# One transposition and split of the keys per head pair, with copies on GpSimd's queue

## The chip, the cores and the metric

The kernel runs on one core of one Trainium2 chip. The metric is the device time of one execution in microseconds (us), stated as the median of several. One core has five engines that each work through their own instruction list in order: TensorE (PE in the rows; its weight loads are PEld), VectorE (DVE), ScalarE (ACT), GpSimd (POOL) and SyncE (SP), which issues most of the transfers. They meet only at semaphores.

## The reference, cut to what matters

Two layers of a trunk over 512 tokens (256 latent and 256 context) of width 1024. In each layer one input projection feeds three branches; two of them are attentions with heads of 64:

```python
z = u @ w_in                                   # columns: qa ka va | qb kb vb | pool | gates
ka = rms_norm(ka.reshape(B, N, NA_HEADS, HEAD_DIM), kn_a)      # 6 heads: 3 pairs
kb = rms_norm(kb.reshape(B, N, GQA_KV_HEADS, HEAD_DIM), kn_b)  # 2 key heads: 1 pair
# branch A: neighbourhood attention of the latent queries over all keys, with a bias
# branch B: grouped attention, three query heads to one key head, rotary on the latent tokens
s = q @ k.T ;  p = softmax(s) ;  y = p @ v
# branch C: pooled means of a 256-wide part of z over windows of 2, 4, 8, 16 tokens, times w_pool
m = ga * (ya @ w_br_a) + gb * (yb @ w_br_b) + gc * (yc @ w_br_c)
```

Then come an output projection and a SwiGLU feed-forward part. So a layer has four pairs of key heads (three of branch A, one of branch B), and the two layers have eight.

## The kernel before, in words

All large products are float32 made of two rounded parts: each operand is split into a high part (rounded by ScalarE) and a low part (the rest, by VectorE), and one product is three matmuls, high by high, low by high, high by low (L227 to L229 for the projections). Weights come by SyncE's transfers as `raw`; ScalarE writes `wh` (L133) and VectorE `wl` (L145). A list of jobs (ORDER) fixes the order of the projections; TensorE's matmuls for them are the main line of the program. Beside it run side generators, of which three are active at a time. After every group of matmuls one of them may take a step; `yield 3` means that it rests for three such ticks. A scheduler then fixes one list for each engine, and an instruction waits until what it needs is there.

The projection of a pair ends with `chunk_end` (L691): GpSimd turns sums of squares into `rs` (L696, L697, a power), and a side generator is added, `prep_na` (L725, branch A) or `prep_kb` (L780, branch B). `prep_na` multiplies keys by `rs` and writes them to `zkn` (L746). TensorE needs the turned keys of each head on both halves of the 128 partitions: a query head is laid out with its high part on one half and its low part on the other (`q_stacks`, L702), so that one matmul over 128 partitions against `ksh` (L876) and one against `ksl` (L877) give all the products. Before the change that layout is made by writing each head twice into `zkn` (two head copies beside each other, the `dup` loop), and by transposing once for each head: `k_stack` (L717) makes four transposes of 128x128 (L720) into one PSUM tile `kt`, then a split into `ksh` (ScalarE, L237) and `ksl` (VectorE, L242, or L239 where there is no scale). `prep_kb` does the same for the key pair of branch B, after norm, gain (L791) and rotation (L774, L777, L796).

GpSimd also does the pooled means (`pool_mix`: sums on L1040, scaling on L1064, subtraction on L1066, whose result ScalarE splits into `plh`, and TensorE multiplies by `wpoolh` into `pool`), rotates the queries of branch B (`prep_qb`: L774, L777, L820), and issues the bias loads `rpb` (L389). Its list, too, is worked off in order.

The attention itself (`attend_x` and `attend_ctx`, L858 and L918) has the score matmuls `s` on L876, L877 and, for the context queries of the first layer, on L926 and L927.

Of the kernel before, what the change touches and what calls it, by code (L numbers as in the profile page):

```python
# [8 lines left out]
F32 = mybir.dt.float32  # L9
F32R = mybir.dt.float32r  # L10
AF = mybir.ActivationFunctionType
ALU = mybir.AluOpType
AX = mybir.AxisListType

P = 128
# [3 lines left out]
TOK = 512  # L19
UNIT = 512  # L20
DEPTH = 2
HD = 64
# [9 lines left out]
ROW_N1, ROW_N2, ROW_PS, ROW_QA, ROW_KA = 48, 56, 64, 66, 67  # L32
# [142 lines left out]
class Trunk:  # L175
# [538 lines left out]
            res.append(t)  # L714
        return res

    def k_stack(self, srcs, scale):  # L717
        ps = self.u("kt")
        for i, s in enumerate(srcs):
            self.nc.tensor.transpose(ps[:, i * P : (i + 1) * P], s, self.ident)  # L720
        k = self.g2([P, TOK], "ks")
        self.split(k[0], k[1], ps, scale)
        return k

    def prep_na(self, l, p, st):  # L725
        nc = self.nc
        rpb = [self.load_bias(l, 2 * p + h) for h in range(2)]
        yield 4
        z, rs = st["z"], st["rs"]
        nq = 2 if l == DEPTH - 1 else 4  # L730
        zq = self.g([P, 4, P], name="zqn")
        zk = [self.g([P, 2, 2, 2, HD], name="zkn") for _ in range(2)]

        def zz(t, c):
            return z[t][:, :, c * P : (c + 1) * P].rearrange("p t (h d) -> p t h d", d=HD)

        def rr(t, c):
            return rs[:, 2 * t : 2 * t + 2, 2 * c : 2 * c + 2].unsqueeze(3).to_broadcast([P, 2, 2, HD])

        for t in range(2):  # L740
            if 2 * t < nq:
                o = zq[:, 2 * t : 2 * t + 2, :].rearrange("p t (h d) -> p t h d", d=HD)
                nc.vector.tensor_tensor(o, zz(t, 0), rr(t, 0), ALU.mult)
        for dup in range(2):
            for t in range(2):
                nc.vector.tensor_tensor(zk[t][:, :, :, dup, :], zz(t, 1), rr(t, 1), ALU.mult)  # L746
        yield 3
        cols = self.cols[l]
        q = self.q_stacks([zq[:, i, :] for i in range(nq)], cols[:, ROW_QA : ROW_QA + 1])
        yield  # L750
        ks = []
        for h in range(2):
            ks.append(
                self.k_stack(
                    [zk[t // 2][:, t % 2, h, :, :].rearrange("p a d -> p (a d)") for t in range(4)],
                    cols[:, ROW_KA : ROW_KA + 1],
                )
            )
            yield
        self.side.add(self.attend_x(l, ("a", p), q, ks, st["v"], rpb))  # L760
        if l < DEPTH - 1:
            self.side.add(self.attend_ctx(l, ("a", p), q, ks, st["v"]))
# [17 lines left out]
    def prep_kb(self, l, p, st):  # L780
        nc = self.nc
        yield 4
        z, rs = st["z"], st["rs"]
        z3 = z.rearrange("p t (h d) -> p (t h) d", d=HD)
        r3 = rs.rearrange("p t h -> p (t h)").unsqueeze(2).to_broadcast([P, 8, HD])
        nc.vector.tensor_tensor(z3, z3, r3, ALU.mult)
        zk = [self.g([P, 2, 2, 2, HD], name="zkn") for _ in range(2)]
        o = zk[1].rearrange("p t h a d -> p (t h) a d")
        x = z[:, 2:4, :].rearrange("p t (h d) -> p (t h) d", d=HD).unsqueeze(2).to_broadcast([P, 4, 2, HD])
        gk = self.gain[:, 1, :].unsqueeze(1).unsqueeze(1).to_broadcast([P, 4, 2, HD])  # L790
        nc.vector.tensor_tensor(o, x, gk, ALU.mult)  # L791
        for tt in range(2):
            t2 = self.rotate(nc.vector, z[:, tt, :], 2, 1, tt)
            x = z[:, tt, :].rearrange("p (h d) -> p h d", d=HD).unsqueeze(2).to_broadcast([P, 2, 2, HD])
            t2 = t2.rearrange("p (h d) -> p h d", d=HD).unsqueeze(2).to_broadcast([P, 2, 2, HD])
            nc.vector.tensor_tensor(zk[0][:, tt, :, :, :], x, t2, ALU.add)  # L796
        yield 3
        ks = []
        for h in range(2):
            ks.append(  # L800
                self.k_stack([zk[t // 2][:, t % 2, h, :, :].rearrange("p a d -> p (a d)") for t in range(4)], 1.0)
            )
            yield
        self.kb = (ks, st["v"])
        self.done.add(("kb", l))

# [715 lines left out]
```

## Time and profile before

| | |
|---|---|
| median of 3 runs | 1257.27 us (1256.89 to 1258.57) |
| profiled execution | 1254.5 us, its span 1252.7 us |
| mean granted TensorE clock in it | 0.983 of full speed |
| TensorE busy | 1205.3 us, 96% of the span |
| VectorE busy | 934.3 us, 75% |
| ScalarE busy | 656.0 us, 52% |
| GpSimd busy | 163.2 us, 13% |

Times in the rows are from the span's start, so 1.8 us of the profiled execution lie outside it. A row of the timeline gives the start, the length and, in brackets, how long the engine had stood idle and which instruction released it. An engine with a high busy share sets the time only where others wait for it, and an engine with a low share can still hold them up at single places.

### The profile page before, as it was taken

How to read it: one execution, taken by the hardware profiler on the slowest of the kernel's cores; microseconds unless marked ns; L12 is line 12 of the kernel's file. 1: busy time of each engine (PE TensorE's matmuls, PEld its weight loads, DVE VectorE, ACT ScalarE, POOL GpSimd, SP SyncE). 2: the span in 40 equal slices, each digit the busy share in tenths (PEclk: the TensorE clock that was granted, in tenths of full speed). 3: DMA queues.
4: the chain of work that ended last, by engine and by line, in shares of the span. 5: the costliest groups of instructions: out<-in, count | busy, mean ns of one | idle time of the engine just before them, and what ended most of it. 6: DMA issues, size and time to landing. Idle time of an engine off the chain costs nothing.

```text
span 1252.7 us, 20829 instructions
## 1 busy us (share of the span) xinstructions
PE 1205.3 (96%) x7307; PEld 1075.9 (86%) x7307; DVE 934.3 (75%) x1736; ACT 656.0 (52%) x1421; POOL 163.2 (13%) x215
## 2 busy tenths in 40 slices
PE   7999999999999889999999999989999999999998
PEld 2788889788887788888887888988999999999998
DVE  5867789999998987776677434778889778755563
ACT  4755588575333543332222333566878667654553
POOL 3253400101100110000000000275011101000000
PEclk9899999999999989999999999989999999999999
DMA  8732244343555444556666333233344565666663
GB/s 291 205 81 69 83 137 129 87 147 122 182 164 188 124 143 135 180 174 226 215 213 213 100 98 102 79 114 92 88 112 113 159 194 161 171 185 184 183 183 97
DMA packets 164612, 185.47 MB, mean 148 GB/s; under 512 B 12840, under 2 KB 148636, under 8 KB 164508
## 3 DMA queue, kind: packets, MB, share of 16 engines
q1 hardware_dynamic: 162700, 181.50, 47.2%
q0 software_dynamic: 1808, 2.66, 1.8%
q8 instruction: 57, 0.93, 0.3%
q14 instruction: 47, 0.39, 0.1%
HBM read 183.05 MB, written 1.05 MB: 147 GB/s over the span
## 4 chain that ended last, share of the span: by engine, by line
PE 73%; DVE 10%; DMA 6%; ACT 5%; issue 4%; POOL 2%; SPq 1%; DVEq 0%; ACTq 0%; POOLq 0%
PE acc L227 22%; PE acc L228 22%; PE acc L229 22%; DMA mraw<-in_w_mod_dram 3%; DVE wl L145 2%; PE y L853 2%; DMA whole<-in_w_mod_dram 2%; ACT wh L133 1%; DVE macc L491 1%; PE pt L899 1%; ACT p L842 1%; DVE xT L1146 1%; PE s L876 1%; PE s L877 1%; DMA raw<-in_w_ff_dram 1%
## 5 line engine op out<-in xcount | busy, mean ns | idle before, releaser
L133 ACT ACTIVATE wh<-raw 128x512 fp32r<-128x512 f32 (+2 forms) x512 | 306.7, 612 | 352.6 <-PE acc L228 251.5
L145 DVE TENSOR_TENSOR wl<-raw,wh 128x512 fp32r<-128x512 f32 (+2 forms) x512 | 343.0, 679 | 164.9 <-ACT wh L133 161.2
L227 PE MATMUL acc<-uh,wh 128*128 128x256 f32 (+1 forms) x1104 | 371.6, 338 | 7.8 <-DVE b L1259 3.6
L229 PE MATMUL acc<-uh,wl 128*128 128x256 f32 (+1 forms) x1104 | 369.7, 336 | 4.7 <-DVE wl L145 4.7
L228 PE MATMUL acc<-ul,wh 128*128 128x256 f32 (+1 forms) x1104 | 369.8, 336 | 1.8 <-DVE ul L591 1.8
L227 PEld LDWEIGHTS acc<-uh,wh 128*128 128x128 f32 x1104 | 211.7, 193 | 28.7 <-issue 3.8
L229 PEld LDWEIGHTS acc<-uh,wl 128*128 128x128 f32 x1104 | 212.4, 193 | 25.1 <-DVE wl L145 4.9
L228 PEld LDWEIGHTS acc<-ul,wh 128*128 128x128 f32 x1104 | 212.8, 193 | 21.3 <-DVE ul L591 2.0
L491 DVE SCALAR_TENSOR_TENSOR macc<-mraw,sf,macc 128x1024 f32<-128x1024 f32 x112 | 143.6, 1289 | 56.2 <-DMA mraw<-in_w_mod_dram 56.2
L227 PE MATMUL acc<-wh,uh 128*128 128x384 f32 (+1 forms) x304 | 100.5, 331 | 4.6 <-ACT uh L1323 4.4
L228 PE MATMUL acc<-wl,uh 128*128 128x384 f32 (+1 forms) x304 | 98.8, 325 | 4.2 <-DVE wl L145 4.2
L229 PE MATMUL acc<-wh,ul 128*128 128x384 f32 (+1 forms) x304 | 98.8, 325 | 0.0
L576 POOL TENSOR_TENSOR ut<-xT,rstd 128x256 f32<-128x256 f32 x30 | 25.0, 862 | 530.3 <-DVE rstd L556 411.9
L227 PE MATMUL acc<-hh,wh 128*128 128x512 f32 (+1 forms) x216 | 75.7, 351 | 0.0
L229 PE MATMUL acc<-hh,wl 128*128 128x512 f32 (+1 forms) x216 | 75.6, 350 | 0.0
L228 PE MATMUL acc<-hl,wh 128*128 128x512 f32 (+1 forms) x216 | 75.5, 350 | 0.0
L227 PEld LDWEIGHTS acc<-wh,uh 128*128 128x128 f32 x304 | 59.2, 195 | 6.1 <-ACT uh L1323 4.5
L228 PEld LDWEIGHTS acc<-wl,uh 128*128 128x128 f32 x304 | 59.4, 195 | 5.5 <-DVE wl L145 4.5
L229 PEld LDWEIGHTS acc<-wh,ul 128*128 128x128 f32 x304 | 59.2, 195 | 0.6 <-DVE ul L1325 0.6
L842 ACT ACTIVATE p<-s,m 128x512 f32<-128x512 f32 (+1 forms) x72 | 44.3, 619 | 13.9 <-DVE m L882 5.5
L227 PE MATMUL acc<-h,wh 128*128 128x256 f32 x176 | 50.3, 286 | 0.0
L228 PE MATMUL acc<-h,wh 128*128 128x256 f32 x176 | 49.8, 283 | 0.0
(279 smaller groups left out, 2180.5 us busy)
## 6 DMA issues: line engine op xcount, KB each, us to landing
raw<-in_w_ff_dram SPq DMA_DIRECT2D x264, 256.0 KB, 3.0
mraw<-in_w_mod_dram SPq DMA_DIRECT2D x80, 512.0 KB, 4.2
raw<-in_w_in_dram SPq DMA_DIRECT2D x112, 256.0 KB, 2.8
raw<-in_w_in_dram SPq DMA_DIRECT2D x144, 64.0 KB, 2.0
whole<-in_w_mod_dram SPq DMA_DIRECT2D x32, 256.0 KB, 5.3
raw<-in_w_out_dram SPq DMA_DIRECT2D x32, 256.0 KB, 3.0
raw<-in_w_in_dram SPq DMA_DIRECT2D x16, 192.0 KB, 2.7
raw<-in_w_br_c_dram SPq DMA_DIRECT2D x8, 256.0 KB, 3.0
```

What stands on the lines that cost most here:

```text
L133: self.nc.scalar.activation(hi[:, :n], self.raw[i][:, :n], AF.Copy)
L145: self.nc.vector.tensor_tensor(lo[:, :n], self.raw[i][:, :n], self.hi[i][:, :n].bitcast(F32), ALU.subtract)
L227: mm(out, st[0], mv[0], start=start, stop=False)
L228: mm(out, st[0], mv[1], start=False, stop=False)
L229: mm(out, st[1], mv[0], start=False, stop=stop)
L491: nc.vector.scalar_tensor_tensor(acc[v], w, c, acc[v], ALU.mult, ALU.add)
L576: eng.tensor_tensor(ts[i][:, 0, :], self.xT[:, kt, c], self.r0[:, c], ALU.mult)
L842: nc.scalar.activation(pt, ps, AF.Exp, scale=-1.0, bias=m, accum_out=s[:, 0:1])
L853: mm(o, st, t[:, kt % 2, :], start=kt == 0 and i == 0, stop=kt == n - 1 and i == 1)
L876: nc.tensor.matmul(ps, st, ks[h][0], start=True, stop=False)
L877: nc.tensor.matmul(ps, st, ks[h][1], start=False, stop=True)
L899: nc.tensor.transpose(ps[:, kt * P : (kt + 1) * P], pr[h, qt][:, kt * P : (kt + 1) * P], self.ident)
```

## The change

`k_stack`, called twice for a pair, becomes `k_stacks`, called once. The keys of the two heads stand side by side in `zkn` (in `prep_kb` in the norm's own tile `z`), each once; four transposes turn both heads at a time, so head 0 lands on partitions 0 to 63 and head 1 on 64 to 127; one split writes `kk`, high and low. After a rest of two ticks eight transfers on GpSimd's queue (L731 of the changed kernel) copy each head's 64x512 block, 128 KB, from `kk` to both halves of its own `ks` tiles: two heads, high and low, two halves. With eight pairs that is 64 transfers and 8.4 MB. Removed are 32 transposes, eight splits (ScalarE and VectorE one each), and half of the doubled writes to `zkn` on VectorE.

```diff
-    def k_stack(self, srcs, scale):
+    def k_stacks(self, srcs, scale):
         ps = self.u("kt")
         for i, s in enumerate(srcs):
             self.nc.tensor.transpose(ps[:, i * P : (i + 1) * P], s, self.ident)
-        k = self.g2([P, TOK], "ks")
-        self.split(k[0], k[1], ps, scale)
-        return k
+        both = self.g2([P, TOK], "kk")
+        self.split(both[0], both[1], ps, scale)
+        yield 2
+        res = []
+        for h in range(2):
+            k = self.g2([P, TOK], "ks")
+            for t, b in zip(k, both):
+                src = b[h * HD : (h + 1) * HD, :].bitcast(F32)
+                for half in range(2):
+                    self.nc.gpsimd.dma_start(out=t[half * HD : (half + 1) * HD, :].bitcast(F32), in_=src)
+            res.append(k)
+        yield
+        return res
...
-        zk = [self.g([P, 2, 2, 2, HD], name="zkn") for _ in range(2)]
+        zk = self.g([P, 4, P], name="zkn")
...
-        for dup in range(2):
-            for t in range(2):
-                nc.vector.tensor_tensor(zk[t][:, :, :, dup, :], zz(t, 1), rr(t, 1), ALU.mult)
+        for t in range(2):
+            o = zk[:, 2 * t : 2 * t + 2, :].rearrange("p t (h d) -> p t h d", d=HD)
+            nc.vector.tensor_tensor(o, zz(t, 1), rr(t, 1), ALU.mult)
...
-        ks = []
-        for h in range(2):
-            ks.append(self.k_stack(...))
-            yield
+        ks = yield from self.k_stacks([zk[:, t, :] for t in range(4)], cols[:, ROW_KA : ROW_KA + 1])
...
-            nc.vector.tensor_tensor(zk[0][:, tt, :, :, :], x, t2, ALU.add)
+            nc.vector.tensor_tensor(z[:, tt, :], z[:, tt, :], t2, ALU.add)
```

Where the copies come to stand in GpSimd's list matters. In the rows below, a name with a number is one buffer of a tile. In the first layer, after the power of the first `rs` of branch B (`rs` of 128x8), GpSimd goes on with the second half of the pooled means; before:

```order
L696 TENSOR_SCALAR rs_1089<-ss_886 128x8
L658 MEMSET ss_1289 128x24
L697 TENSOR_TENSOR rs_1089<-rs_1089,mhalf 128x8
L1040 TENSOR_TENSOR s_173_1150<-vp_874 128x271
L1040 TENSOR_TENSOR s_174_1151<-s_173_1150 128x268
```

The same place of GpSimd's list in the changed kernel (x2 is two instructions alike, one for each half of the partitions; L1034 is the old L1040):

```order
L696 TENSOR_SCALAR rs_1086<-ss_886 128x8
L658 MEMSET ss_1290 128x24
L697 TENSOR_TENSOR rs_1086<-rs_1086,mhalf 128x8
L731 DMA ksh_1110<-kkh_1083 64x512 x2
L731 DMA ksl_1111<-kkl_1084 64x512 x2
L731 DMA ksh_1116<-kkh_1083 64x512 x2
L731 DMA ksl_1117<-kkl_1084 64x512 x2
L1034 TENSOR_TENSOR s_173_1150<-vp_874 128x271
L1034 TENSOR_TENSOR s_174_1151<-s_173_1150 128x268
```

The eight copies of the first pair have come between the power and the second half of the pooled means.

TensorE's list at the product of that second half with `wpoolh`, before:

```order
L720 MATMUL kt_1232<-ident,zkn_1217 128x128
L720 MATMUL kt_1241<-ident,zkn_1217 128x128
L227 MATMUL pool_1250<-plh_1148,wpoolh_882 128x512
L227 MATMUL acc_1296<-wh_1179,uh_124 128x384
L228 MATMUL pool_1250<-pll_1149,wpoolh_882 128x512
L229 MATMUL pool_1250<-plh_1148,wpooll_883 128x512
```

And in the changed kernel:

```order
L721 MATMUL kt_1230<-ident,zk_888 128x128
L229 MATMUL acc_1296<-wh_1179,ul_125 128x384
L227 MATMUL pool_1258<-plh_1148,wpoolh_882 128x512
L721 MATMUL kt_1230<-ident,zk_888 128x128 x3
L228 MATMUL pool_1258<-pll_1149,wpoolh_882 128x512
L229 MATMUL pool_1258<-plh_1148,wpooll_883 128x512
```

The product stands where it stood: right after the first transposes of branch B's keys, and ahead of all that follows on TensorE.

In the second layer, at the first pair of branch A, GpSimd's list has the rotation of two query tiles and then waits for the next `ss`; before:

```order
L774 TENSOR_TENSOR rot_1120_8891<-zqn_1119_8889,rope_1050_8332 128x12x16 [waits DVE_49]
L774 TENSOR_TENSOR rot_1120_8891<-zqn_1119_8889,rope_1050_8332 128x12x16
L777 TENSOR_TENSOR zqn_1119_8889<-zqn_1119_8889,rope_1050_8332 128x384 [waits Pool_49]
L820 TENSOR_TENSOR zqn_1119_8889<-zqn_1119_8889,rot_1120_8891 128x384 [waits Pool_49]
L696 TENSOR_SCALAR rs_1151_9086<-ss_1105_8824 128x8 [waits DVE_49]
L697 TENSOR_TENSOR rs_1151_9086<-rs_1151_9086,mhalf_81 128x8 [waits Pool_49]
```

In the changed kernel (L777, L780 and L814 are the old L774, L777 and L820; what an instruction waits for stands in brackets, DMASW being an earlier transfer of this queue):

```order
L777 TENSOR_TENSOR rot_1119_8892<-zqn_1118_8890,rope_1049_8333 128x12x16
L780 TENSOR_TENSOR zqn_1118_8890<-zqn_1118_8890,rope_1049_8333 128x384 [waits Pool_49]
L814 TENSOR_TENSOR zqn_1118_8890<-zqn_1118_8890,rot_1119_8892 128x384 [waits Pool_49]
L731 DMA ksh_1128_8980<-kkh_1126_8964 64x512 [waits DMASW3_49,Activation_49]
L731 DMA ksh_1128_8980<-kkh_1126_8964 64x512 [waits DMASW4_49]
L731 DMA ksl_1129_8981<-kkl_1127_8965 64x512 [waits DMASW5_49,DVE_49]
L731 DMA ksl_1129_8981<-kkl_1127_8965 64x512 [waits DMASW6_49]
L731 DMA ksh_1130_8986<-kkh_1126_8964 64x512 [waits DMASW7_49]
```

The copies stand behind the last rotation. On TensorE the first score matmul of this pair had 24 projection matmuls between the first `kt` and itself before, and has 36 of them now.

## Rows read from the trace of the kernel before

**Rows 1.** The page: engine totals, and shares of the chain that ended last

```profile
PE 1205.3 (96%) x7307; PEld 1075.9 (86%) x7307; DVE 934.3 (75%) x1736; ACT 656.0 (52%) x1421; POOL 163.2 (13%) x215
...
PE 73%; DVE 10%; DMA 6%; ACT 5%; issue 4%; POOL 2%; SPq 1%; DVEq 0%; ACTq 0%; POOLq 0%
```

**Rows 2.** Groups by form (busy us, mean ns, idle before) of what the change thins

```profile
L720 PE MATMUL kt<-ident,zkn 128*128 128x128 f32 x64 | 10.5, 281 | 2.5 <-DVE zkn L746 2.0 <-DVE zkn L796 0.5
L746 DVE TENSOR_TENSOR zkn<-z,rs 128x256 f32<-128x256 f32 x24 | 12.9, 592 | 0.0
L242 DVE SCALAR_TENSOR_TENSOR ksl<-kt,cols,ksh 128x512 fp32r<-128x512 f32 x12 | 8.9, 748 | 0.9 <-ACT ksh L237 0.6
```

**Rows 3.** Issues on GpSimd by line: ns min/median/max; the last row is landing

```profile
L376 POOL DMA_DIRECT2D wpool<-in_w_pool_dram x8: 518/529/560, 42.4 to 818.1; - x8
DMA to landing us min/median/max: 2.2/2.4/3.6
L389 POOL DMA_DIRECT2D rpb<-in_rpb_a_dram x24: 592/606/683, 44.6 to 951.6; - x24
DMA to landing us min/median/max: 3.2/4.2/6.4
```

**Rows 4.** TensorE's timeline behind the first pair's second four transposes, first layer

```profile
89.35 0.50 PE L227 MATMUL acc<-uh,wh 128*128 128x512 f32 x1 [0.63 <-DVE v L239]
```

**Rows 5.** GpSimd's timeline there, and ScalarE's split of the pooled means

```profile
89.97 0.20 POOL L696 TENSOR_SCALAR rs<-ss 128x8 f32<-128x8 f32 x1 [6.09 <-DVE ss L687]
...
91.95 0.63 POOL L1040 TENSOR_TENSOR s<-vp 128x271 f32<-128x271 f32 x1
...
103.11 1.07 POOL L1066 TENSOR_TENSOR r<-r,vp 128x256 f32<-128x256 f32 x1
104.22 0.42 ACT L237 ACTIVATE plh<-r 128x256 fp32r<-128x256 f32 x1 [3.02 <-POOL r L1066]
```

**Rows 6.** TensorE's timeline at the pooled product

```profile
105.33 0.41 PE L720 MATMUL kt<-ident,zkn 128*128 128x128 f32 x2 [0.46 <-DVE zkn L796]
105.50 0.47 PE L227 MATMUL pool<-plh,wpoolh 128*128 128x512 f32 x1
```

**Rows 7.** TensorE after an idle stretch; window: length, busy (count), clock, transfers' share, GB/s

```profile
830.09 0.69 PE L228 MATMUL acc<-wl,uh 128*128 128x384 f32 x1 [4.21 <-DVE wl L145]
830.00:835.00 5.00, 4.91 (x15) 0.51 0.38 110
```

**Rows 8.** TensorE's timeline at the first pair of the second layer

```profile
857.92 0.44 PE L720 MATMUL kt<-ident,zkn 128*128 128x128 f32 x2 [1.26 <-DVE zkn L746]
859.05 0.69 PE L720 MATMUL kt<-ident,zkn 128*128 128x128 f32 x2 [0.69 <-DVE zkn L746]
...
862.10 0.67 PE L720 MATMUL kt<-ident,zkn 128*128 128x128 f32 x4
862.52 0.36 PE L227 MATMUL acc<-wh,uh 128*128 128x256 f32 x1
...
864.04 0.40 PE L876 MATMUL s<-ksh,qs 128*128 128x512 f32 x1
```

**Rows 9.** VectorE and GpSimd there

```profile
854.83 4.16 DVE L746 TENSOR_TENSOR zkn<-z,rs 128x256 f32<-128x256 f32 x4
850.85 0.64 POOL L389 DMA_DIRECT2D rpb<-in_rpb_a_dram  x1
851.51 2.94 POOL L697 TENSOR_TENSOR rs<-rs,mhalf 128x16 f32<-128x16 f32 x1
...
861.94 1.01 POOL L820 TENSOR_TENSOR zqn<-zqn,rot 128x384 f32<-128x384 f32 x1
```

**Rows 10.** TensorE's timeline at the second pair of branch A, first layer

```profile
238.05 0.60 PE L720 MATMUL kt<-ident,zkn 128*128 128x128 f32 x4
...
244.42 0.39 PE L876 MATMUL s<-ksh,qs 128*128 128x512 f32 x1
244.65 0.39 PE L877 MATMUL s<-ksl,qs 128*128 128x512 f32 x1
```

More of the change, by code (lines that the diff above doesn't have):

```diff
@@ L750, in prep_na @@
         yield
-        ks = []
-        for h in range(2):
[L753 to L758, printed above, removed]
-            yield
+        ks = yield from self.k_stacks([zk[:, t, :] for t in range(4)], cols[:, ROW_KA : ROW_KA + 1])
         self.side.add(self.attend_x(l, ("a", p), q, ks, st["v"], rpb))
@@ L786, in prep_kb @@
         nc.vector.tensor_tensor(z3, z3, r3, ALU.mult)
[L787 to L791, printed above, removed]
+        gk = self.gain[:, 1, :].unsqueeze(1).to_broadcast([P, 4, HD])
+        x = z[:, 2:4, :].rearrange("p t (h d) -> p (t h) d", d=HD)
+        nc.vector.tensor_tensor(x, x, gk, ALU.mult)
         for tt in range(2):
             t2 = self.rotate(nc.vector, z[:, tt, :], 2, 1, tt)
-            x = z[:, tt, :].rearrange("p (h d) -> p h d", d=HD).unsqueeze(2).to_broadcast([P, 2, 2, HD])
-            t2 = t2.rearrange("p (h d) -> p h d", d=HD).unsqueeze(2).to_broadcast([P, 2, 2, HD])
-            nc.vector.tensor_tensor(zk[0][:, tt, :, :, :], x, t2, ALU.add)
+            nc.vector.tensor_tensor(z[:, tt, :], z[:, tt, :], t2, ALU.add)
         yield 3
[L798 to L803, printed above, removed]
+        ks = yield from self.k_stacks([z[:, t, :] for t in range(4)], 1.0)
         self.kb = (ks, st["v"])
```

## The prediction

> **What bounds the kernel now.** I read the engine totals first, then the chain that ended last, then the timelines around the places that the diff touches. TensorE is busy 96% of the span and holds 73% of the chain [rows 1]. So the kernel is bound by TensorE almost everywhere: work taken from TensorE is time gained, work taken from VectorE or ScalarE counts only where TensorE waits for them, and GpSimd, busy 13%, counts only where something queued behind a new instruction is waited for. That last point is the one that the reader should keep in mind: the average says nothing about a single place in GpSimd's list.
>
> The profiled execution took 1254.5 us, span 1252.7; the median of the runs is 1257.27, which is 2.8 us more. I make the sum as a difference on the profiled execution and add it to the median.
>
> **What is removed.** Four transposes cost TensorE the time from their start to the next matmul's start, 862.52 - 862.10 = 0.42 us [rows 8]; 32 fewer are eight times that, 3.4 us at most. The 0.42 counts in full where TensorE would otherwise go on at once. At the first pair of the first layer it does not: behind the second four TensorE waits 0.63 us for VectorE's `v` anyway [rows 4], and that wait ends when it ends. I count nothing there, put the first pair of the second layer into its own term below, and 6 x 0.42 = 2.5 us for the other six pairs. VectorE loses twelve of its 24 writes of 592 ns and eight splits of about 748 ns, 13 us in all [rows 2], ScalarE eight splits; these are hidden beside TensorE's matmuls, except that TensorE waits 2.0 us for the writes on L746 [rows 2], and 1.26 + 0.69 of it in one place [rows 8]. That gain is in the term of that place.
>
> **What is added.** Eight transfers for a pair on GpSimd's queue. An issue holds GpSimd: the power on L697 starts at 851.51, just as the issue before it ends (850.85 + 0.64) [rows 9]. An issue takes 529 ns for `wpool` and 606 for `rpb`, at most 683 [rows 3], so eight take 4.2 to 5.5 us; I take 0.57 each, 4.6 us, between the two, as the copies have regular rows like `wpool` but more bytes. From issue to landing the two lines show 2.4 and 4.2 us at the median, 2.2 to 6.4 at the ends [rows 3]; I take 3.0 for 128 KB inside the chip's own memory, nearer to `wpool`, whose rows are as many. No row shows a copy of this kind, so the ends stay for the range. TensorE's score matmuls now wait for these landings, and GpSimd's next instructions for the issues. I went through the eight pairs and found two where this is late.
>
> **First layer, first pair.** GpSimd's list has the eight copies between the power, which ends when the pooled sums start at 91.95, and the second half of the pooled means, 91.95 to 104.18 [rows 5]. What the copies read is there by then: its transposes stand in TensorE's list ahead of the matmul at 89.35 [rows 4], and the split's low part, 748 ns after a high part of about that length, is done by 90.9. So the pooled means are pushed back by the issues, 4.6 us. ScalarE makes `plh` from them the moment they end, 104.22, in 0.42 [rows 5], so now it is ready at about 104.64 + 4.6 = 109.2. TensorE's pooled product started at 105.50 [rows 6] and now starts at 109.25: 3.75 us later. TensorE stands ready for it from about 105.2: it was free at 105.33 - 0.46 = 104.87 [rows 6] and has a transposition and one matmul ahead of it. Nothing behind the product can pass it, as TensorE's list is in order. Standing idle for 4 us costs a second time: after 4.21 us of idleness the granted clock in the next 5 us was 0.51, the lower of its levels (1.2 of 2.4 GHz), and 15 matmuls took 4.91 us [rows 7], of which 49% is 2.4 us lost. Term: 3.75 + 2.4 = +6.1 us. Low end: eight issues of 0.52, and an `rs` that comes 1.9 us earlier since VectorE has two writes and a split less ahead of it (2 x 592 + 748 ns, [rows 2]; GpSimd idled 6.09 before `rs` [rows 5]), and no loss of clock: 4.2 - 1.9 - 0.9 = +1.4 (the 0.9 being the slack between 104.64 and 105.50). High end: eight of 683 ns, 4.6 + 2.4 = +7.0.
>
> **Second layer, first pair.** First the gain. VectorE's four writes of `zkn` took 4.16 us from 854.83 [rows 9], 1.04 each beside GpSimd's rotation; two are done at 856.9, so TensorE's first `kt`, at 857.92 after 1.26 us of idleness, starts at about 856.9, and the second wait of 0.69 goes [rows 8]. The slow clock that followed goes too: the twelve matmuls and two transposes from 859.05 to 862.10 took 3.05 us, the twelve and four from 862.10 to 864.04 1.94 [rows 8]. With 0.42 for the transposes and 36 matmuls at (864.04 - 862.52) / 12 = 0.127 us, TensorE reaches the first score matmul at 856.9 + 0.42 + 4.6 = 861.9. In the old order it would have done as much work at 864.04 + 12 x 0.127 = 865.6: a gain of 3.7 us. Then the loss. The copies stand behind the rotation, whose last instruction ends at 861.94 + 1.01 = 862.95 [rows 9]. The second copy, which the high score matmul needs, is issued at 863.5 and lands at 866.5: TensorE idles 4.6 us. The fourth, issued at 864.7, lands at 867.7, after two score matmuls of 0.23 us: 0.7 more. With 2.4 us of clock the loss is 7.7. Term: 7.7 - 3.7 = +4.0 us. Low end, landing 2.2 and 1.1 us of clock (what the old place lost, 3.05 - 1.94): 3.8 + 0.5 + 1.1 - 3.7 = +1.7. High end, landing 6.4: 8.0 + 0.7 + 2.4 - 3.7 = +7.4.
>
> **The other six pairs.** They have room. At the second pair of branch A in the first layer, `kt` stood at 238.05 and the first score matmul at 244.42 [rows 10]; now 36 matmuls of 0.23 us (244.65 - 244.42) stand between them, 8.3 us. Transposes 0.60, the split 0.75, two issues and the landing are 0.60 + 0.75 + 0.6 + 3.0 = 5.0. At the other pairs there is as much work or more in between, and GpSimd has nothing before the copies that lasts. Nothing but the 2.5 us is counted.
>
> **Sum.** 6.1 + 4.0 - 2.5 = +7.6 us: 1262.1 for the profiled execution, 1264.9 for the median. With both low ends +0.6, 1257.9; with both high ends +11.9, 1269.2.
>
> **Rivals.** *Hidden after all, a faster kernel.* At the pooled product the copies cost nothing if `rs` comes about 3.7 us earlier, 4.6 less the slack of 0.9. VectorE's lighter list is worth 1.9 at the mean rates and 2.8 if its two writes would have run at the slow rate of 1.04; GpSimd's idle 6.09 us speaks for it, the `rs` that still waits for TensorE's own projection speaks against it. At the second layer the rotation would have to be freed of VectorE's writes and end 1.5 us earlier, with landing at 2.2: TensorE idles some 2 us, loses 1.1 of clock, and the gain of 3.7 pays for it. Then the six pairs' 2.5 us are left, with some tenths: -3 us, 1254.3. The point from which it decides is whether GpSimd starts the second half of the pooled means by 92.9. Half of this, one place hidden and one not, ends near zero: 1257.5.
>
> *The copies are slow, a still slower kernel.* If a copy lands after 6.4 us, as the slowest `rpb` did [rows 3], the second layer's first pair costs 3.4 more, and the chain of 5.0 above becomes 8.4 against 8.3, the low part later still: some 1.5 us each at three of the other pairs. 7.6 + 3.4 + 4.5 = +15.5, 1272.8. Issues held up by VectorE would act in the same way. Against it stand 24 issues within 592 to 683 ns, though VectorE is busy 75% of the span [rows 1, 3].
>
> The Trainium skill has a rule that speaks for this second rival: its page "SBUF — State Buffer", section "SBUF: two separate sides", says that a transfer from GpSimd's queue waits for its descriptors while VectorE runs an operation that takes the shared port pair, some 3100 ns in place of 620. By that figure, eight copies would take an estimated 25 us, and the time would be past 1290. The same page, in "Who interferes with whom", leaves two-input operations such as VectorE's weight splits out of that rule, and the 24 issues above agree; no row here shows a copy beside an operation of the other kind.
>
> **How the numbers follow.** Forecast, both places late: 0.56. Slow copies: 0.14. One place hidden, near zero: 0.12. Both hidden: 0.18. A measurement of this kernel can tell about 0.2%, 2.5 us, from no change. Slower by more than that takes the first two, 0.70; within it 0.12; faster 0.18. The range goes down to the hidden case, 1254.0, and up to the slow copies, 1273.0; what is left out is about a tenth below, where more than the six pairs' gain comes through, and less than a tenth above.
>
> **What would show it.** In the changed kernel's timeline: eight issues of 0.5 to 0.7 us between L697 and the pooled sums; TensorE idle some 4 us before `pool`, released by `plh`; at the first pair of the second layer, idle some 4 to 5 us before the first score matmul, released by a transfer; a granted clock near 0.5 right after both; no such wait at the other six pairs. The prediction is wrong if GpSimd goes on while its issues are written, if the pooled product comes at 105.5 all the same, or if score matmuls wait at other pairs.

## The result, and the profile after

The changed kernel takes 1274.63 us (median of 4 runs, 1270.81 to 1275.65) against 1257.69 for the kernel before: 1.0144 times as long, interval 1.0127 to 1.016, 17 to 18 us more. The forecast was 1264.9 with a range up to 1273.0. The direction came as forecast; the forecast's +7.6 us is under half of what came, and the median lies 1.6 us above the range. The profiled execution took 1274.27, its span 1272.5.

The totals of the page, the copies' queue, and the head of the chain that ended last, of the changed kernel:

```profile
PE 1209.2 (95%) x7275; PEld 1077.2 (85%) x7275; DVE 923.2 (73%) x1716; ACT 651.4 (51%) x1413; POOL 194.2 (15%) x279
...
q0 software_dynamic: 4880, 11.05, 4.5%
...
PE 69%; DVE 10%; DMA 8%; ACT 5%; issue 3%; POOL 3%; SPq 1%; DVEq 0%; ACTq 0%; POOLq 0%
```

Against [rows 1] TensorE has its 32 transposes less, yet its share of the chain fell from 73% to 69%: it waits more. The 64 copies, all of line L731, as that line's answer shows them:

```profile
L731 POOL DMA_DIRECT2D ksh<-kkh x32: 518/535/614, 91.6 to 981.9; - x32
L731 POOL DMA_DIRECT2D ksl<-kkl x32: 518/518/541, 92.7 to 982.9; - x32
...
who waited for it (us, times):
  PE s L870: 5.4, 1
  PEld s L871: 1.2, 1
  PE s L871: 0.5, 1
...
DMA to landing us min/median/max: 2.2/3.7/7.3
```

Issues hold GpSimd for 0.52 us, a little under the 0.57 taken; landings have a median of 3.7 us against the 3.0 taken. Only one score matmul waits long for a landing, 5.4 us. That alone cannot make 17.

**First layer, first pair.** GpSimd's timeline (start, duration, line, operation), then TensorE's. This answers to [rows 5] and [rows 6]:

```profile
89.98 1.67 POOL L697 TENSOR_TENSOR rs<-rs,mhalf 128x8 f32<-128x8 f32 x1
...
94.77 1.03 POOL L731 DMA_DIRECT2D ksl<-kkl  x2
95.82 0.65 POOL L1034 TENSOR_TENSOR s<-vp 128x271 f32<-128x271 f32 x1
```

```profile
105.11 0.33 PE L721 MATMUL kt<-ident,zk 128*128 128x128 f32 x1 [1.21 <-DVE zk L795]
107.74 0.79 PE L227 MATMUL pool<-plh,wpoolh 128*128 128x512 f32 x1 [2.12 <-ACT plh L237]
```

The second half of the pooled means starts at 95.82 in place of 91.95, behind eight issues, and the pooled product at 107.74 in place of 105.50. Ahead of it TensorE also waits 1.21 us for VectorE's `zk`.

**Second layer, first pair.** GpSimd, then TensorE, answering to [rows 8] and [rows 9]:

```profile
870.32 1.32 POOL L814 TENSOR_TENSOR zqn<-zqn,rot 128x384 f32<-128x384 f32 x1
871.58 1.12 POOL L731 DMA_DIRECT2D ksh<-kkh  x2
872.67 1.05 POOL L731 DMA_DIRECT2D ksl<-kkl  x2
```

```profile
875.51 1.20 PE L870 MATMUL s<-ksh,qs 128*128 128x512 f32 x2 [5.42 <-DMA ksh<-kkh]
877.23 1.19 PE L871 MATMUL s<-ksl,qs 128*128 128x512 f32 x2 [0.53 <-DMA ksl<-kkl]
...
890.90 0.66 PE L893 MATMUL pt<-ident,p 128*128 128x128 f32 x4 [1.75 <-ACT p L836]
...
892.88 0.58 PE L227 MATMUL acc<-uh,wh 128*128 128x256 f32 x1 [0.68 <-ACT gate L1105]
```

The copies stand behind the rotation, and TensorE idles until they land, as forecast. The last two rows were not: fifteen microseconds later TensorE waits for ScalarE's softmax and gate. The stretches, with TensorE's busy time and count, granted clock, and the transfers' share:

```profile
105.00:115.00 10.00, 7.76 (x27) 0.66 0.32 82
870.00:875.00 5.00, 0.09 (x1) 0.98 0.55 157
875.00:885.00 10.00, 8.96 (x44) 0.67 0.37 92
885.00:890.00 5.00, 4.16 (x34) 1.00 0.14 38
890.00:900.00 10.00, 8.25 (x43) 0.66 0.26 69
```

A mean of 0.66 over 10 us is about two thirds of that time at the lower of the two levels, 1.2 of 2.4 GHz. Around the idle stretch the clock falls once, is back at 1.00 from 885 to 890, and falls again around the two short waits.

**Where the 20 us of the profiled spans lie.** I summed, for each trace, the time with no matmul running, up to the last matmul (idle), and over windows of 5 us what a granted clock under full speed took, 5 x (1 - clock). The rest is matmul work at full clock and some 3 us behind the last matmul. A slow clock in an idle stretch counts in both columns, and each row is one execution, so a microsecond or two between two rows means little. The last two columns split the idle time where the edits act; the middle of the program, 330 to 845 us, has no head pair of the changed kind, and its idle time differs by up to 6 us and its clock by 7 among kernels all the same.

| kernel | span | idle | clock | rest | idle, first layer (85 to 330) | idle, second layer (from 845) |
|---|---|---|---|---|---|---|
| before | 1252.7 | 44.2 | 20.5 | 1188.0 | 6.6 | 8.4 |
| after | 1272.5 | 60.0 | 27.2 | 1185.2 | 11.4 | 16.7 |
| e3, no copies | 1249.0 | 44.6 | 17.6 | 1186.8 | 6.7 | 6.9 |
| e6, SyncE's queue | 1266.9 | 52.7 | 27.1 | 1187.0 | 7.3 | 14.1 |
| e11, copies not read | 1264.9 | 55.2 | 22.2 | 1187.5 | 13.6 | 11.1 |
| e13, half of their columns | 1256.8 | 47.6 | 23.9 | 1185.3 | 9.5 | 7.2 |
| e14, not read, SyncE | 1256.1 | 48.7 | 20.4 | 1187.0 | 6.9 | 11.1 |

The transposes' gain is there, though only roughly: the rest is lower by 2.8 here and by 0.5 to 2.7 in the five other kernels with as many fewer. What the change loses is idle time, 15.8 more, of which 13.1 in the last two columns, and 6.7 of clock, most of it in the second layer. One part is not the copies' doing: between 640 and 700 us the starts of like projection matmuls show the changed kernel falling 2.4 us further behind the kernel before, and e9 and e10 below, which have no copies, do so by 2.2 and 4.6.

### The profile page after: what moved, and what is told of

It is laid out like the page before. It is cut to its first block, busy times and chain, and to the rows that moved or that the text cites. A ratio compares the mean times of both kernels' runs of the same rounds, so it can differ in the third digit from the quotient of the medians.

```text
span 1272.5 us, 20904 instructions
## 1 busy us (share of the span) xinstructions
PE 1209.2 (95%) x7275; PEld 1077.2 (85%) x7275; DVE 923.2 (73%) x1716; ACT 651.4 (51%) x1413; POOL 194.2 (15%) x279
## 4 chain that ended last, share of the span: by engine, by line
PE 69%; DVE 10%; DMA 8%; ACT 5%; issue 3%; POOL 3%; SPq 1%; DVEq 0%; ACTq 0%; POOLq 0%
PE acc L227 21%; PE acc L228 21%; PE acc L229 21%; DMA mraw<-in_w_mod_dram 6%; DVE wl L145 2%; DVE macc L491 2%; PE y L847 2%; DMA whole<-in_w_mod_dram 2%; ACT wh L133 1%; ACT p L836 1%; PE pt L893 1%; DVE xT L1140 1%; POOL s L1034 1%; ACT p L838 1%; DMA ksl<-kkl 1%
## 5 line engine op out<-in xcount | busy, mean ns | idle before, releaser
L227 PE MATMUL acc<-uh,wh 128*128 128x256 f32 (+1 forms) x1104 | 372.4, 339 | 10.1 <-DVE b L1253 3.6
L836 ACT ACTIVATE p<-s,m 128x512 f32<-128x512 f32 (+1 forms) x72 | 44.2, 619 | 16.7 <-DVE m L876 10.3
L227 PE MATMUL acc<-h,wh 128*128 128x256 f32 x176 | 50.3, 286 | 0.0
L229 PE MATMUL acc<-h,wl 128*128 128x256 f32 x176 | 49.8, 283 | 0.0
```

Source lines behind the costliest of these rows:

```text
L227: mm(out, st[0], mv[0], start=start, stop=False)
L229: mm(out, st[1], mv[0], start=False, stop=stop)
L836: nc.scalar.activation(pt, ps, AF.Exp, scale=-1.0, bias=m, accum_out=s[:, 0:1])
```

## The experiments

Ratios are to the kernel before, on the same chip, with the 95% interval; 0.001 is 1.26 us.

| run | what is run | median us | ratio |
|---|---|---|---|
| e1_two_places | only the first pair of each layer uses copies | 1269.31 | 1.0108 [1.0082, 1.0133] |
| e2_six_others | only the other six | 1262.96 | 1.0043 [1.0023, 1.0063] |
| e3_no_copies | spread left out | 1249.46 | 0.9943 [0.9927, 0.9958] |
| e4_copies_unused | kernel before and copies nobody reads | 1285.91 | 1.0229 [1.0207, 1.0251] |
| e5_unused_behind | the same, behind the hand-on | 1276.29 | 1.016 [1.0138, 1.0182] |
| e6_sync_queue | copies from SyncE's queue | 1266.8 | 1.0082 [1.0061, 1.0104] |
| e7_half_copies | four copies for a pair | 1265.08 | 1.008 [1.0055, 1.0105] |
| e8_engines | ScalarE and VectorE write both halves | 1263.75 | 1.0052 [1.0034, 1.0071] |
| e9_steps_only | kernel before, e5's extra step without copies | 1256.55 | 0.9997 [0.9982, 1.0012] |
| e10_act_dup | kernel before, ScalarE doubles `zkn` | 1252.1 | 0.9969 [0.9954, 0.9984] |
| e11_unread | all copies, nobody reads them | 1267.65 | 1.0093 [1.007, 1.0116] |
| e12_unread_64 | e11 with 64 of 512 columns | 1255.91 | 1.0009 [0.9993, 1.0025] |
| e13_unread_256 | e11 with 256 columns | 1257.2 | 1.0011 [0.9986, 1.0036] |
| e14_unread_sync | e11 from SyncE's queue | 1258.64 | 1.0029 [1.0013, 1.0046] |

### Two places or all eight: e1, e2

```diff
+        old = kind in ("na", "kb") and not self.use_new(l, kind, p)
+    def use_new(self, l, kind, p):
+        return kind == "na" and p == 0          # e1
+        return not (kind == "na" and p == 0)    # e2
```

> Only the first pair of branch A in each layer uses the copies; the other six pairs stay as before. Theory 1 (the loss is made at the two places where the copies queue on GpSimd): the trace of the changed kernel shows TensorE 5.4 us behind after the pooled product and 8.3 us lost at the second layer's first pair, so about +13 us, 1270. Theory 2 (the extra traffic slows other transfers everywhere): a quarter of the copies, about +4 us, 1262. Wait of the first score matmul of the second layer for a transfer: theory 1 about 5 us.

> The complement: six pairs use the copies, the first pair of branch A in each layer stays as before. Theory 1: 24 transposes fewer and no wait, -2.5 us, 1255. Theory 2 (traffic): three quarters of the copies, about +12 us, 1270. A rest that belongs to neither (the 2.6 us that TensorE waits near 658 us for the modulation's reduction in the changed kernel) would show as +1 to +4 us.

The two places cost 13.6 us and the other six 5.4, where -2.5 was forecast. They add to 19, near the whole change's 18, so the forecast failed in both: the two places cost 3.5 more than the 10.1 of the sum, and the six 8 more. In e2 one pair waits for a landing after all, on TensorE:

```profile
897.09 0.47 PE L952 MATMUL s<-ksl,qs 128*128 128x512 f32 x1 [1.35 <-DMA ksl<-kkl]
```

That is 1.35 of 8 us. Its second layer idles 12.3 us against 8.4 before, most of the rest in waits for ScalarE's `p`, `pth` and `gate`: together 4.6 us against 2.0 before. What the other 4 us of e2's miss are was not traced.

### Removal without copies: e3

```diff
-        res = []
-        for h in range(2):
...
-            res.append(k)
+        res = [both, both]
```

> One transposition and split per pair, but no copies at all: the score matmuls read the undivided keys, so the spread of each head over both halves is left out and the scores are other numbers. It measures what the removed work is worth. Theory 1: 0.42 us for each of seven pairs and 2.7 us at the second layer's first pair (the measured fall of the lag there), -5.5 us, 1252. Rival (the new order of the instructions costs by itself): no gain or a loss, 1257 to 1261.

What the change removes is worth 7.2 us (5.3 to 9.2); the copies therefore cost 0.0201, 25 us. The question became what the 25 are made of.

### Copies that nobody reads, in the kernel before: e4, e5, e9

```diff
+    def k_more(self, ks):
+        yield 2
+        for h in range(2):
+            d = self.g2([P, TOK], "kx")
+            for t, b in zip(d, ks[h]):
+                src = b[h * HD : (h + 1) * HD, :].bitcast(F32)
+                for half in range(2):
+                    self.nc.gpsimd.dma_start(out=t[half * HD : (half + 1) * HD, :].bitcast(F32), in_=src)
+        yield from self.k_more(ks)   # e4: ahead of the hand-on to attention, with a last yield; e5: behind it
+        yield 2                      # e9: this alone
```

> The kernel before, with the same eight 64x512 transfers per pair added after the split, into tiles that nobody reads. No wait for a landing, but all of the issues and the traffic. Theory 1: GpSimd's list is delayed by 4.2 us at the pooled means, which costs TensorE 3 to 5 us there, and nothing elsewhere: 1261 to 1263. Theory 2 (traffic): +10 us or more, 1268 to 1274, spread over the span.

> As in the run with unused copies, but the eight transfers are put behind the point at which the pair's attention is handed on, so that they delay no step of it; nobody reads what they write. Theory A (the loss of the unused copies came from attention being handed on three steps later): only the delay of the pooled means in the first layer is left, 1260 to 1264. Theory B (issues on GpSimd and traffic cost by themselves): 1280 or more.

> The control to the unused copies behind the attention: the kernel before with the same rest of two ticks in the side generator and no transfers. Theory A (issues on GpSimd's queue and traffic make the 19 us): 1256 to 1259, like the kernel before. Theory B (the steps of the side generators, by which the scheduler orders everything else, make them): 1270 or more.

Copies that no matmul waits for cost 29 and 20 us, above both theories' times in e4 and between the two in e5; e5's extra step, without the copies, costs nothing. So waiting for landings is not the main price. But these runs did not say what is: the order of instructions on all engines moved too, and e4 delays the hand-on of attention.

### Other ways to spread: e6, e7, e8

```diff
-                    self.nc.gpsimd.dma_start(out=t[half * HD : (half + 1) * HD, :].bitcast(F32), in_=src)
+                    self.nc.sync.dma_start(out=t[half * HD : (half + 1) * HD, :].bitcast(F32), in_=src)     # e6
+                self.nc.gpsimd.dma_start(out=t[other, :].bitcast(F32), in_=t[own, :].bitcast(F32))          # e7
+            for o in (own, other):
+                nc.scalar.activation(k[0][o, :], ps[own, :], AF.Copy, scale=sc)                             # e8
```

> The changed kernel with its 64 copies issued by SyncE in place of GpSimd. Theory A (GpSimd's list is what makes the copies late and the pooled means wait): both waits go, no idle of 2 us before the pooled product and none of 5 us before the second layer's scores, and the time falls to the one without copies plus 2 to 5 us, 1252 to 1255. Theory B (it is the landing time of about 4 us, or the copies' wait holding SyncE's weight loads): 1262 or more, with the score matmuls or the weight splits waiting for transfers.

> The changed kernel with half the copies: each head's split writes its own half of the partitions directly (two splits of 64 partitions for a pair in place of one of 128), and GpSimd copies only the other half, four transfers for a pair. If the cost goes with the number of issues, half of the 25 us between the changed kernel and the one without copies is left: 1262. If it goes with the time to landing, which is the same for the first copies, the first pair of the second layer still waits some 4 us: 1268 to 1272.

> One transposition for a pair, and no transfers: ScalarE writes the high part of each head to both halves of the partitions and VectorE the low part (four instructions of 64 partitions each in place of one of 128). If the loss is all in the copies, this comes near the kernel without copies, 1250 to 1253. If the copied work is needed off ScalarE and VectorE (two instructions more on each than before for a pair, some 1.4 us each), the score matmuls come later: 1256 to 1260.

With SyncE's queue the wait for `plh` at the first place is gone, and the second place waits less; the copies land sooner. TensorE at the second place, and the landings:

```profile
869.50 0.70 PE L870 MATMUL s<-ksh,qs 128*128 128x512 f32 x2 [2.91 <-DMA ksh<-kkh]
870.58 1.14 PE L871 MATMUL s<-ksl,qs 128*128 128x512 f32 x2 [0.25 <-DMA ksl<-kkl]
```

```profile
DMA to landing us min/median/max: 2.3/2.4/3.3
```

This takes 0.0062 off the change, 7.8 us: the price of GpSimd's part in it. Ten remain, more than theory A had. Half as many copies (e7) gain about as much, yet the first score matmul there still waits 4.37 us. Without any transfer (e8) the time stays above the kernel before, and above both of its theories. e8 has four writes on ScalarE and VectorE for each head where the kernel before has two, and TensorE waits 1.5 us for one of them (`ksl`) in the second layer; the rest of its loss was not traced.

### Copies with no reader, by length and queue: e11 to e14

```diff
-        return res
+        return [both, both]                                    # e11 to e14: the scores read kk
-                src = b[h * HD : (h + 1) * HD, :].bitcast(F32)
+                src = b[h * HD : (h + 1) * HD, :64].bitcast(F32)   # e12 (and the out); :256 in e13
+                    self.nc.sync.dma_start(...)                    # e14, full length
```

> The changed kernel with all its transfers at the same places in GpSimd's list, but the score matmuls read the undivided keys, so nobody waits for a landing (the spread over both halves is left out of the scores, which are other numbers). Theory A (the waits for landings, and the later scores that follow from them, are the larger part): the 25 us between the changed kernel and the one without copies shrink to the pooled means' 5 us, 1253 to 1256. Theory B (issues and traffic are the larger part): 1265 or more.

> As the run in which nobody reads the copies, but each of the 64 transfers moves 64 columns in place of 512 (16 KB in place of 128 KB; 1 MB in all): as many issues, an eighth of the bytes. Theory I (the issues on GpSimd make the 18 us over the kernel without copies): 1265 to 1268 again. Theory T (the bytes): 1250 to 1257. Theory L (the scheduler's lists, which it orders by the length that it gives to a transfer): 82 matmuls stand elsewhere than in the kernel without copies, where 147 did with the full transfers, so in between, 1256 to 1262.

> The same with 256 columns, 64 KB a transfer, 4.2 MB in all. Its lists on all engines are the same, instruction for instruction, as with 64 columns, so the difference to that run is the bytes alone. Theory T: 3 us or more above it. Theories I and L: within 1.5 us of it.

> The unread copies at full size, issued by SyncE: GpSimd issues nothing, the bytes are the same. Theory I: GpSimd's issues being gone, 1249 to 1253. Theory T or L: 1258 or more.

The issues alone (theory I) had e12 at 1265 or more; it took 1255.91. The bytes alone (theory T) had e13 at 3 us or more above e12; it is 1.3 above by the medians, 0.0002 by the ratios. The order of the lists (theory L) is what e12 to e14 leave, with e12 just under its range. These four and e3, e6 and the change itself form a grid, and three prices come out of it, each twice or more (each difference is uncertain by 3 to 4 us):

| price | differences of ratios | us |
|---|---|---|
| scores wait for landings | e11 to after 0.0051; e14 to e6 0.0053 | 6.4, 6.7 |
| issued on GpSimd, not on SyncE | e14 to e11 0.0064; e6 to after 0.0062; e3 to e13 0.0068 | 8.0, 7.8, 8.5 |
| full length | e13 to e11 0.0082; e3 to e14 0.0086 | 10.3, 10.8 |

6.5 + 8 + 10.5 = 25, the price of the copies. That they add up proves nothing, as the steps lead from e3 to the change; what supports the prices is that the two ways there agree one by one. Each step also moves some matmuls in TensorE's list, so a price is that of an edit with the new order that it brings. (e3 stands for no issue at all, so its two differences hold whatever SyncE's issues or the short copies cost besides.)

At least half of the GpSimd price arises at the first place: from 95 to 120 us TensorE falls behind by 4.3 us more in e13 than in e3, 4.5 more in e11 than in e14 and 5.9 more in the change than in e6 (starts of like matmuls). The rest of it was not traced. e12, with copies of an eighth, has the same wait for `plh` there, and e14 none:

```profile
106.12 0.33 PE L721 MATMUL kt<-ident,zk 128*128 128x128 f32 x1 [1.20 <-DVE zk L795]
108.75 0.79 PE L227 MATMUL pool<-plh,wpoolh 128*128 128x512 f32 x1 [2.12 <-ACT plh L237]
```

The price of the length is the odd one: nobody reads those copies. Bytes as such are not it between 64 and 256 columns: e12 and e13 have the same instructions in the same order on every engine and four times the bytes between them, and differ by 0.0002. From 256 to 512 columns the order changes. The scheduler that lays the program out reckons with the length of transfers, and with longer ones it places other work elsewhere: against e3, some 80 of 7254 matmuls stand elsewhere in e12 and e13, 150 in e11, 120 in e14, 200 in the change. (The counts depend somewhat on how two lists are matched.) The count by itself prices nothing: in e9 more than 500 stand elsewhere than in the kernel before, and its time is unchanged. What counts is what moves, and where. ScalarE's order at the second layer's first pair, e13 first, then e11 (the numbers behind the names are buffers):

```
L237 ACTIVATE kkh_8964<-kt_8959,cols_113 128x512
L133 ACTIVATE wh_8998<-raw_8766 128x512
L681 ACTIVATE zk_8827<-acc_8830 128x128
...
L681 ACTIVATE zk_8827<-acc_8833 128x128
L133 ACTIVATE wh_9098<-raw_8768 128x512
L836 ACT_TABLE_LOAD
```

```
L237 ACTIVATE kkh_8964<-kt_8959,cols_113 128x512
L133 ACTIVATE wh_8998<-raw_8766 128x512
L133 ACTIVATE wh_9098<-raw_8768 128x512
L681 ACTIVATE zk_8827<-acc_8830 128x128
...
L681 ACTIVATE zk_8827<-acc_8833 128x128
L133 ACTIVATE wh_9129<-raw_8840 128x512
L836 ACT_TABLE_LOAD
```

In e11 a split of a weight, `wh_9098`, stands ahead of the copies of `zk` out of the accumulators, and a further one, `wh_9129`, ahead of the softmax. What that does is in ScalarE's timeline of e11, then TensorE's:

```profile
868.53 0.63 ACT L133 ACTIVATE wh<-raw 128x512 fp32r<-128x512 f32 x1 [0.74 <-PE acc L229]
873.68 0.63 ACT L133 ACTIVATE wh<-raw 128x512 fp32r<-128x512 f32 x1 [4.52 <-DMA raw<-in_w_in_dram]
874.22 0.26 ACT L681 ACTIVATE zk<-acc 128x128 f32<-128x128 f32 x1
...
877.16 0.63 ACT L133 ACTIVATE wh<-raw 128x512 fp32r<-128x512 f32 x1 [1.50 <-PE acc L228]
877.81 1.28 ACT L836 ACT_TABLE_LOAD   x1
```

```profile
875.58 0.36 PE L227 MATMUL acc<-uh,wh 128*128 128x256 f32 x1 [1.47 <-DVE v L239]
886.61 0.66 PE L893 MATMUL pt<-ident,p 128*128 128x128 f32 x4 [1.75 <-ACT p L836]
...
888.59 0.39 PE L227 MATMUL acc<-uh,wh 128*128 128x256 f32 x1 [0.77 <-ACT gate L1105]
```

ScalarE stands 4.52 us at that split and 1.50 at the next, everything behind it comes late, and TensorE waits 1.47, 1.75 and 0.77 us. e14, planned for full length too but with GpSimd free, has the same waits, here TensorE's:

```profile
866.90 0.36 PE L227 MATMUL acc<-uh,wh 128*128 128x256 f32 x1 [1.47 <-DVE v L239]
877.92 0.66 PE L893 MATMUL pt<-ident,p 128*128 128x128 f32 x4 [1.73 <-ACT p L836]
879.90 0.39 PE L227 MATMUL acc<-uh,wh 128*128 128x256 f32 x1 [0.78 <-ACT gate L1105]
```

A weight that lands late beside the copies would be a rival for e11's 4.52. e14 speaks against it: ScalarE stands as long at the same split there, and what releases it is a matmul, not a transfer:

```profile
865.01 0.63 ACT L133 ACTIVATE wh<-raw 128x512 fp32r<-128x512 f32 x1 [4.54 <-PE acc L229]
```

In e13 ScalarE begins its `zk` at 867.16, as soon as the split ahead of it is done, and TensorE's waits come to 0.59 for `p`, 0.77 for `pth` and 0.17 for `gate`, none for `v`: 1.5 in all against 4.2 in e11 (its `pth` costing 0.17):

```profile
866.44 0.63 ACT L133 ACTIVATE wh<-raw 128x512 fp32r<-128x512 f32 x1 [0.74 <-PE acc L229]
867.16 0.28 ACT L681 ACTIVATE zk<-acc 128x128 f32<-128x128 f32 x1
```

The changed kernel has the split at the same position, and waits there longer, since TensorE itself stands waiting for the copies; the rows of `pt` and `gate` at 890.90 and 892.88 above are the consequence:

```profile
870.13 0.63 ACT L133 ACTIVATE wh<-raw 128x512 fp32r<-128x512 f32 x1 [2.24 <-PE acc L229]
...
881.45 0.63 ACT L133 ACTIVATE wh<-raw 128x512 fp32r<-128x512 f32 x1 [9.35 <-PE acc L228]
882.10 1.28 ACT L836 ACT_TABLE_LOAD   x1
```

So the traces lead to the re-planned order as a cause in the second layer, where TensorE idles about 4 us more in both kernels (11.1 against 7.2 in e13 and 6.9 in e3), 2.7 of it in the waits above. The rest of the 10.5 is not settled line by line: in e11 much of it lies in the first layer (13.6 against 9.5, of it one wait of 2.36 for `ptl` at 277.14), in e14 part of it in the middle's clock. Nor was a full-length copy run in e13's order, so a price of the last 256 columns' bytes isn't excluded by itself, though the 192 before them had none that could be measured. How e4's and e5's totals divide stays open too.

### A version that beats both: e10

```diff
-        for dup in range(2):
-            for t in range(2):
-                nc.vector.tensor_tensor(zk[t][:, :, :, dup, :], zz(t, 1), rr(t, 1), ALU.mult)
+        for t in range(2):
+            nc.vector.tensor_tensor(zk[t][:, :, :, 0, :], zz(t, 1), rr(t, 1), ALU.mult)
+        for t in range(2):
+            nc.scalar.activation(zk[t][:, :, :, 1, :], zk[t][:, :, :, 0, :], AF.Copy)
```

> The kernel before with one edit: the second of the doubled writes of the keys of branch A is a copy made by ScalarE instead of a product made by VectorE. If what the change gains at the second layer's first pair is VectorE's shorter list there (TensorE waited 1.95 us and then lost 1.7 us of clock), this gains 1 to 3 us without any transfer: 1254 to 1256. If ScalarE's copies come as late, no change.

The kernel before, with the second of the doubled writes made by ScalarE: 0.9969, 3.9 us faster. VectorE, ScalarE and TensorE at the second layer's first pair:

```profile
856.52 1.90 DVE L745 TENSOR_TENSOR zkn<-z,rs 128x256 f32<-128x256 f32 x2
...
857.71 0.42 ACT L747 ACTIVATE zkn<-zkn 128x256 f32<-128x256 f32 x1 [3.32 <-DVE zkn L745]
...
858.92 0.44 PE L720 MATMUL kt<-ident,zkn 128*128 128x128 f32 x2 [0.30 <-ACT zkn L747]
```

TensorE's wait of 1.26 + 0.69 us [rows 8] becomes 0.30: part of what the change removes, had without a transfer.

## Why the prediction was right in direction and wrong in size

- **What bounds.** Right: 32 transposes less on TensorE show as 0.5 to 2.8 us less in the table's rest, and what was lost was TensorE's waiting and granted clock.
- **What is removed.** Right. The sum had 2.5 for six pairs and 3.7 at the second layer's first pair, 6.2 in all; e3 measured 7.2, with 6.2 inside its interval.
- **An issue's price.** Eight took 4.2 us (91.61 to 95.82), the low end of the 4.2 to 5.5.
- **First layer, first pair (+6.1).** Right mechanism: the eight issues, the pooled sums behind them, idle before `pool` released by `plh`, the lower clock behind it. Idle was 2.12 and 1.21 against 3.75: the issues took 0.4 less, the power ended 0.3 earlier, and the pooled means took 11.4 us in place of 12.2. The clock lost 3.4 (10 us at 0.66), some 0.5 of it while TensorE stood idle, against 2.4. TensorE was 5.4 us behind the kernel before at 120 us, and 3.5 by 225, where the kernel before lost clock that the changed one did not.
- **Second layer, first pair (+4.0).** The mechanism of gain and wait came as worked out: TensorE made up 2.7 us by VectorE's shorter list (3.7 forecast) and idled 5.42 + 0.53 for the copies (4.6 + 0.7). The net was +8.3: the step that failed is that the loss was taken to end at the score matmuls. The waits for `p` and `gate` behind them, and a second fall of the clock from 890 to 900, worth 3.4, were not in the sum.
- **The other six pairs (-2.5).** Here the forecast failed outright: +5.4 in e2. The step "Nothing but the 2.5 us is counted" took the room between `kt` and the scores as the only question. One landing was late by 1.35, and waits for ScalarE's `p`, `pth` and `gate` in the second layer were 2.6 longer than before; the rest of the 8 us stays open.
- **The missing term.** The prediction kept the order of all other work as it was, outside the places it looked at. Full-length copies change that order, and their length costs some 10.5 of the 25 us that the copies cost. About 4 us of idle time in the second layer were followed to the new order; that the whole 10.5 comes from it is not shown.
- **The rivals.** Hidden after all: excluded, GpSimd started the second half at 95.82, not by 92.9. Slow copies: its time, 1272.8, was nearest to the 1274.63, but by luck and not by its mechanism: the slowest landing was 7.3 us, yet late landings are worth only 6.5 us in all, and no issue took over 0.614. The Trainium skill's page "SBUF — State Buffer", section "SBUF: two separate sides", gives some 3100 ns for a transfer from GpSimd's queue beside a VectorE copy that holds the port pair the two engines share. The 64 issues at 518 to 614 ns, with VectorE busy 73%, do not show it, though no run here set a copy beside such an operation on purpose.

## What to carry to other kernels

Where a scheduler lays out the program, compare the orders of the whole program on the engine that the bound one waits for, not only at the edit: a transfer that nobody reads can cost as much as one that is waited for, here in part because other work was moved on its account. Price such an edit by a grid (work removed alone; transfers without a reader; another queue; another length) rather than by one sum. And do not stop the sum at the first late matmul: follow the engine that it feeds, whose lateness comes back, here fifteen microseconds later.

## What the runs showed of the hardware

The same 128 KB copies land after 2.3, 2.4 and 3.3 us (least, median, most) from SyncE's queue, after 2.2, 3.7 and 7.3 from GpSimd's. Waits for single instructions of 1.75 and 0.68 us, two microseconds apart, went with a granted clock of 0.66 over 10 us (890 to 900) in the changed kernel, a dearer loss than the waits; in e11 waits of 1.75 and 0.77 us, as far apart, went with 0.83 (888 to 898), half of that loss. Copies with four times the bytes at an unchanged order (e12, e13) cost nothing that ten runs of each could measure: 0.0002, uncertain by some 0.003.
